# A hybrid mixer and expert network: context first, all its experts gathered row by row, value rows summed on PE

## The chip, the cores and the metric

The kernel runs on one core of one Trainium2 chip. The metric is the device time of one execution in microseconds, the median of the runs.

## The reference

Two layers act on 256 latent tokens `x` and 256 context tokens `ctx`, of 1024 channels each. A layer has a mixer and a PEER block. The second layer updates the latents only; its context enters through the keys and values.

```python
def mixer_sublayer(x, ctx, mod_x, mod_c, lp, rope, update_ctx):
    hx = modulate(rmsnorm(x, lp['g_norm1']), sh, sc)
    hc = modulate(rmsnorm(ctx, lp['g_norm1']), csh, csc)
    k_c, v_c = mla_kv(hc @ lp['w_in'][:, :KV_IN], lp, None)
    k_x, v_x = mla_kv(hx @ lp['w_in'][:, :KV_IN], lp, rope)
    ...
    a_x = latent_attention(q_x, concat(k_c, k_x), concat(v_c, v_x))
    x = x + gt * branch_merge(a_x, zf_x, zc_x, zg_x, lp)   # attention, FFT, convolution
    if update_ctx:
        a_c = softmax_attend(mla_q(cq_c, lp, None), k_c, v_c)
        ctx = ctx + cgt * branch_merge(a_c, zf_c, zc_c, zg_c, lp)

def peer_ffn(h, w_query, sub_keys, u_tab, v_tab):   # per token
    q = h @ w_query                                  # 8 heads x 2 x 64
    ...                                              # top 16 of 128 x 128 keys per head
    act = gelu(dot(u_tab[eid], h)) * softmax(best)   # 128 experts of 16384 a token
    return sum(act * v_tab[eid])
```

In layer 0 the context's mixer reads nothing of the latents, so it can go first; the latents' attention needs the context's keys and values.

## The kernel before

Channels lie on the partitions, tokens on the free axis; the residual `xT` and the normed input `hT` (a high and a low part) hold 512 columns, the context's 256 ahead of the latents' 256. Every weight tile of 512 KB is loaded by `raw` (SP's queue), rounded to its high part by ACT (`whi`, L237) and its low part is made by POOL, or by DVE for every third tile (`wlo`, L243). `mm3` (L257 to L259) does three matmuls for each chunk of 128.

The program runs in this order. `mixer(0)` does both streams at once, with 512 columns to a matmul: norm, convolution input, projections, keys and queries (`keys`), attention (`attend`), the branches' merge (`merge1`) and the output projection (`project`). The modulation (`adaln`, 12 parts; a part loads 4 MB in four tiles `wm` and multiplies each in four matmuls of 32 output columns, tile `ada`) is woven into the mixers: 2 parts first, 6 more in layer 0's mixer, 4 in layer 1's. Then `peer(0)`: queries, and for each of the four token tiles of 128 `retrieve` (L781), the top-16 search on DVE. Each token has 128 chosen experts. For the first token tile (`GATHER`) the chosen rows are fetched: `rows` (L856) lets POOL issue an indirect DMA for each of the 128 slots, 128 rows of 4 KB at a time, first of `u_tab`, which DVE multiplies with the token's input and sums (`dot`, L888; against `hnear` in PSUM, or `htok` in SBUF later), then of `v_tab`, which DVE scales and adds to `acc` (L901). There are five row buffers. The other 384 tokens are computed densely, all 16384 experts for each: `dense_u` computes scores tile by tile (`su`; 92 of 128 expert tiles are written to memory, the rest is computed in the value stage), `gates` builds a matrix of gate weights from one-hot products (`pw`, L951), and `dense_v` multiplies scores and gates (`xa`, L1028; split to `xh`, `xl` in L251 and L252) and sums the value rows in PSUM (`yacc`, six banks). Layer 1's mixer has 256 latent columns and 512 keys, and its PEER is dense for the 256 latents.

What sets the order: `weave` (L1059) interleaves generators by counts, and the counts stand in tables (`SPILL`, `END`, `PREP`, `FETCH`). A scheduler then orders each engine's instructions; `behind` and `pace` keep fetches and dots from moving ahead of the dense work that they were written beside.

Of the kernel before, what the change touches and what calls it, by code (L numbers as in the profile page):

```python
# [21 lines left out]
D = 1024  # L22
# [20 lines left out]

GATHER = (128, 0)
# [102 lines left out]
def body(ctx: ExitStack, tc, nc, a, out):  # L149
# [8 lines left out]
    pss = ctx.enter_context(tc.tile_pool(name="pss", bufs=2, space=PSUM))  # L158
    dram = ctx.enter_context(tc.tile_pool(name="dram", bufs=1, space=DRAM))


    last = ExitStack()
    banks = []

    def more_banks():
        last.close()
        psh = last.enter_context(pool_("psh", 2, space=PSUM))
        banks[:] = [ps, ps, psh, psh]

    def fewer_banks():  # L170
        last.close()
        banks[:] = [ps]
        return last.enter_context(pool_("psn", space=PSUM))
# [5 lines left out]
    ctx.callback(last.close)  # L179
    more_banks()  # L180
# [3 lines left out]

    def sm(name="sm"):
        return pss.tile([P, 512], F32, name=name, tag="sm")
# [46 lines left out]
    def split(r, n=D, lo_eng=None):  # L233
# [6 lines left out]
        if lo_eng is None:  # L240
            turn[0] += 1
            lo_eng = V if turn[0] % 3 == 0 else G
# [68 lines left out]
    def adaln(l, parts, pool, depth):  # L311


        acc = tp("ada")
# [102 lines left out]
    def head_norm_rope(pool, src, g, tile_idx, rope, name):  # L417

        sq = pool.tile([P, H, QKH], F32, name=name + "_hsq", tag="hsq", bufs=2)
# [7 lines left out]
        if rope:  # L427
# [3 lines left out]
            r = pool.tile([P, H, ROPE], F32, name=name + "_rot", tag="hrot", bufs=1)  # L431
# [20 lines left out]
    ADA1 = (6, 4, 4, 2, 4)  # L452

    def mixer(l, lay):
        both = l < L - 1
        streams = (0, 1) if both else (1,)
        q0 = 0 if both else NS
        nT = T - q0
        wt = a["wt"][l]
        macc = lay.tile([P, 8, nT], F32, name="macc")  # L460
        bra = lay.tile([P, 4, nT], F32, name="bra")
        bs = [lay.tile([P, 4, nT], F32R, name="bs%d" % k) for k in range(2)]

        def proj(i, cols=(q0, T), src=None, n=P):
            r = raw(wt[i] if src is None else src, 8 * n)
            w = split(r, 8 * n)
            p = mm("proj")
            for c in range(8):
                mm3(p[:n, :cols[1] - cols[0]], chunk(w, c, n), part(hT, c, cols), c == 0, c == 7)
            return p  # L470

        def gate(i):

            pz = proj(i)
            sg = lay.tile([P, nT], F32, name="gate", tag="gate", bufs=3)
            S.activation(out=sg, in_=pz[:, :nT], func=AF.Tanh, scale=0.5)
            return sg

        def branch(w, k0, x, xc, nk):
            pb = mm("pb")  # L480
            for k in range(nk):
                mm3(pb[:, :nT], chunk(w, k0 + k), part(x, xc + k, (0, nT)), k == 0, k == nk - 1)
            return pb[:, :nT]

        def conv(cp, up):
            cv = cp.tile([P, 2, nT], F32, name="cv")
            ns = len(streams)
            for c in range(2):
                o = cv[:, c].rearrange("p (s t) -> p s t", s=ns)
                for k in range(CW):  # L490
                    src = up[:, c, streams[0]:, k:k + NS]
# [6 lines left out]
            for c in range(2):  # L498
                PE.matmul(pmn[:, :nT], lhsT=ones, rhs=cv[:, c], start=c == 0, stop=c == 1)
            yield  # L500
            for c in range(2):
                V.scalar_tensor_tensor(out=cv[:, c], in0=pmn[:, :nT], scalar=-1.0 / 256, in1=cv[:, c], op0=ALU.mult, op1=ALU.add)
            ss = squares(cp, lambda c: cv[:, c], 2, nT, "cln")
            yield
            rs = tokstat(cp, ss, nT, 1.0 / 256, "cln")
            yield
            bc = spread(cp, rs, nT, "cln")
            for c in range(2):
                V.tensor_tensor(out=cv[:, c], in0=cv[:, c], in1=bc[:, :nT], op=ALU.mult)
# [3 lines left out]
        def fourier(fp, zf):  # L513
# [4 lines left out]
            for s in streams:  # L518
                for c in range(2):
                    o = s * NS - q0  # L520
                    zz = fp.tile([P, 2, 2, P], F32, name="zz", bufs=2)
                    for t in range(2):
                        p = mm("zc")
                        PE.matmul(p[:, :2 * P], lhsT=zf[:, c, o + t * P:o + (t + 1) * P], rhs=dftc, start=True, stop=True)
                        S.copy(out=zz[:, t], in_=p[:, :2 * P].rearrange("p (a b) -> p a b", a=2))
                    p = mm("zt")
                    for k in range(4):
                        PE.matmul(p[:, :NS], lhsT=zz[:, k // 2, k % 2], rhs=dftt[:, k // 2, k % 2], start=k == 0, stop=k == 3)
                    split_to(bs[0][:, c, o:o + NS], bs[1][:, c, o:o + NS], p[:, :NS])
                    yield  # L530
# [15 lines left out]
        def latents(ki, tmp):  # L546

            ckv = ki.tile([P, T], F32, name="ckv")
            kr = ki.tile([P, T], F32, name="krt")
            cq = ki.tile([P, 2, nT], F32, name="cq")  # L550
            p = proj(W_CKV, (0, T))
            ss = tmp.tile([P, T], F32, name="ckv_ss", tag="sq")
            S.activation(out=ss, in_=p, func=AF.Square)
            S.activation(out=ckv, in_=p, func=AF.Identity, scale=gckv[:, l])
            yield
            p = proj(0, (0, T), a["w_kr"][l], ROPE)
            S.copy(out=kr[:ROPE], in_=p[:ROPE])
# [646 lines left out]
```

## Time and profile before

| | |
|---|---|
| median of 3 runs | 2885.29 us (2884.65 to 2888.88) |
| profiled execution | 2882.8 us, its span 2881.0 us |
| mean granted clock | 0.981 |
| DMA | 675.67 MB, 235 GB/s in the mean |
| ACT busy | 1206.3 us, 42% |

Durations below come from the profiled execution, which is 2.5 us under the median. A matmul's listed duration is longer than the distance from its start to the next one's, since matmuls are pipelined; the distance is what counts. A matmul of plain 32-bit numbers shows as two records.

### The profile page before, as it was taken

The numbers are of one execution on the slowest core, as the hardware profiler recorded it, in microseconds if no ns is written. First come the engines' busy times: TensorE is split into PE (matmuls) and PEld (weight loads), VectorE is DVE, ScalarE is ACT, GpSimd is POOL, SyncE is SP. The second block draws the span as 40 slices with busy tenths as digits, with TensorE's granted clock in tenths as the row PEclk, the third lists the DMA queues.
The fourth block names the chain that finished last, engine by engine and source line by source line (L and its number), as shares of the span: only waits on it lengthen the run. The fifth ranks groups of instructions, "written<-read, shape, count | busy, mean of one in ns | idle before, by whom it ended". The sixth has DMA issues, their size and how long they took to land.

```text
span 2881.0 us, 43347 instructions
## 1 busy us (share of the span) xinstructions
PE 2741.1 (95%) x16144; PEld 2391.0 (83%) x16144; DVE 2170.9 (75%) x3907; ACT 1206.3 (42%) x1940; POOL 1498.0 (52%) x789
## 2 busy tenths in 40 slices
PE   7889999978999999999999998899999999999999
PEld 3467679877999998998788886678898999998887
DVE  4665437999989728999999996865398965667665
ACT  2144435432434443333333333455444554445543
POOL 2232235564666658899655563435443436665443
PEclk9999999988999999999999999999999999999999
DMA  8622144465778769999999995235465768667884
GB/s 330 249 73 80 37 132 132 154 217 200 288 269 296 284 245 354 323 319 316 366 354 349 352 321 219 92 110 209 148 204 197 249 226 291 211 206 254 292 291 141
DMA packets 263347, 675.67 MB, mean 235 GB/s; under 512 B 20192, under 2 KB 109408, under 8 KB 260320
## 3 DMA queue, kind: packets, MB, share of 16 engines
q1 hardware_dynamic: 210720, 467.63, 47.9%
q0 software_dynamic: 36864, 134.23, 12.7%
q10 hardware_dynamic: 15552, 71.05, 6.5%
q8 instruction: 126, 2.06, 0.3%
q14 instruction: 85, 0.70, 0.1%
HBM read 600.74 MB, written 72.09 MB: 234 GB/s over the span
## 4 chain that ended last, share of the span: by engine, by line
PE 77%; DVE 14%; DMA 4%; issue 2%; ACT 1%; POOL 1%; SPq 0%; DVEq 0%; ACTq 0%; POOLq 0%
PE yacc L257 10%; PE yacc L258 10%; PE yacc L259 10%; PE su L257 8%; PE su L259 8%; PE su L258 8%; PE pw L951 5%; PE proj L257 3%; PE proj L258 3%; PE proj L259 3%; PE ada L324 1%; DVE oh L827 1%; DVE wlo L243 1%; PE sc L628 1%; PE po L652 1%
## 5 line engine op out<-in xcount | busy, mean ns | idle before, releaser
L243 POOL TENSOR_TENSOR wlo<-wraw,whi 128x1024 fp32r<-128x1024 f32 (+1 forms) x466 | 1115.8, 2399 | 1055.1 <-ACT whi L237 1024.3
L237 ACT CAST whi<-wraw 128x1024 fp32r<-128x1024 f32 (+2 forms) x676 | 676.5, 1006 | 710.7 <-PE su L258 344.7
L257 PE MATMUL su<-hT,whi 128*128 128x384 f32 (+1 forms) x2048 | 643.7, 314 | 17.6 <-ACT psc L794 14.2
L259 PE MATMUL su<-hT,wlo 128*128 128x384 f32 (+1 forms) x2048 | 638.2, 312 | 11.8 <-DVE wlo L243 9.3
L258 PE MATMUL su<-hT,whi 128*128 128x384 f32 (+1 forms) x2048 | 640.0, 313 | 0.0
L257 PE MATMUL yacc<-whi,xh 128*128 128x512 f32 x1280 | 498.1, 390 | 7.6 <-ACT xh L251 7.6
L258 PE MATMUL yacc<-wlo,xh 128*128 128x512 f32 x1280 | 499.9, 391 | 0.0
L259 PE MATMUL yacc<-whi,xl 128*128 128x512 f32 x1280 | 497.0, 390 | 0.4 <-DVE xl L252 0.4
L257 PEld LDWEIGHTS su<-hT,whi 128*128 128x128 f32 x2048 | 393.4, 192 | 22.5 <-ACT psc L794 14.7
L259 PEld LDWEIGHTS su<-hT,wlo 128*128 128x128 f32 x2048 | 392.1, 192 | 13.5 <-DVE wlo L243 9.7
L243 DVE TENSOR_TENSOR wlo<-wraw,whi 128x1024 fp32r<-128x1024 f32 x210 | 305.4, 1455 | 129.9 <-ACT whi L237 126.3
L258 PEld LDWEIGHTS su<-hT,whi 128*128 128x128 f32 x2048 | 393.4, 192 | 3.0
L251 ACT CAST xh<-xa 128x384 fp32r<-128x384 f32 (+1 forms) x256 | 117.6, 460 | 585.8 <-DVE xa L1028 264.7
L257 PEld LDWEIGHTS yacc<-whi,xh 128*128 128x128 f32 x1280 | 240.6, 188 | 56.6 <-ACT xh L251 8.9
L259 PEld LDWEIGHTS yacc<-whi,xl 128*128 128x128 f32 x1280 | 240.4, 188 | 51.2 <-DVE xl L252 1.4
L258 PEld LDWEIGHTS yacc<-wlo,xh 128*128 128x128 f32 x1280 | 240.6, 188 | 47.9 <-POOL wlo L243 0.4
L252 DVE TENSOR_TENSOR xl<-xa,xh 128x384 fp32r<-128x384 f32 (+1 forms) x256 | 203.4, 796 | 94.9 <-ACT xh L251 94.7
L901 DVE SCALAR_TENSOR_TENSOR acc<-rows,act,acc 128x1024 f32<-128x1024 f32 x127 | 236.6, 1863 | 6.2 <-DMA rows<-in_v_tab,eidi 5.5
L862 POOL DMA_INDIRECT rows<-in_v_tab,eidi x128 | 160.2, 1252 | 154.2 <-DVE acc L901 119.5
L257 PE MATMUL proj<-hT,whi 128*128 128x512 f32 (+2 forms) x544 | 195.0, 361 | 14.0 <-ACT hT L251 10.0
L1028 DVE TENSOR_TENSOR xa<-snew,wrd 128x256 f32<-128x256 f32 (+1 forms) x80 | 132.0, 1652 | 92.3 <-ACT snew L1004 59.1
L259 PE MATMUL proj<-hT,wlo 128*128 128x512 f32 (+2 forms) x544 | 188.7, 347 | 1.2 <-POOL wlo L243 1.2
(273 smaller groups left out, 4226.1 us busy)
## 6 DMA issues: line engine op xcount, KB each, us to landing
wraw<-in_u_t SPq DMA_DIRECT2D x256, 512.0 KB, 4.3
wraw<-in_v_tab SPq DMA_DIRECT2D x256, 512.0 KB, 5.4
wraw<-in_wt SPq DMA_DIRECT2D x114, 512.0 KB, 3.8
wm<-in_w_mod SPq DMA_DIRECT2D x48, 1024.0 KB, 7.0
wd<-wst ACTq DMA_DIRECT2D x20, 2048.0 KB, 8.9
wrd<-wd SPq DMA_DIRECT2D x32, 768.0 KB, 11.1
sd<-sst ACTq DMA_DIRECT2D x46, 384.0 KB, 3.7
srd<-sd SPq DMA_DIRECT2D x46, 384.0 KB, 6.4
```

What stands on the lines that cost most here:

```text
L237: ins = S.copy(out=hi[:, :n], in_=r[:, :n])
L243: ins = lo_eng.tensor_tensor(out=lo[:, :n], in0=r[:, :n], in1=hi[:, :n].bitcast(F32), op=ALU.subtract)
L251: S.copy(out=hi, in_=src)
L252: return eng.tensor_tensor(out=lo, in0=src, in1=hi.bitcast(F32), op=ALU.subtract)
L257: PE.matmul(dst, lhsT=wh, rhs=xh, start=first, stop=False)
L258: PE.matmul(dst, lhsT=wh, rhs=xl, start=False, stop=False)
L259: return PE.matmul(dst, lhsT=wl, rhs=xh, start=False, stop=last)
L324: PE.matmul(acc[32 * g:32 * g + 32], lhsT=cond[:, c + g // 2, 6 - 2 * k:38 - 2 * k], rhs=w[:, g // 2, g % 2 * 512:(g % 2 + 1) * 512], star ...
L862: ins = G.indirect_dma_start(out=r, out_offset=None, in_=a[tab], in_offset=bass.IndirectOffsetOnAxis(ap=eid[:, k:k + 1], axis=0))
L901: return V.scalar_tensor_tensor(out=acc, in0=v, scalar=act[:, k:k + 1], in1=acc, op0=ALU.mult, op1=ALU.add)
L951: ins = PE.matmul(pw[:, t * NK:(t + 1) * NK], lhsT=oj[:, :, t], rhs=gg[:, k, :, t], start=k == 0, stop=k == 1)
L1028: V.tensor_tensor(out=x.rearrange("p (g t) -> p g t", t=TG), in0=got.pop(i).rearrange("p (g t) -> p g t", t=TG), in1=w[:, :, i % WB], op=A ...
```

## The change

1. `mixer` does one stream. Layer 0's context goes first, alone, with the ten parts of the modulation that are not needed ahead of it beside it (`run_beside` and `tick`: a step of the other work for so many microseconds of PE work, by the table `RATE`). Then the latents' mixer, beside which stand the context's queries, the retrieval of the first context tile and its 128 fetches of U rows. All weights of layer 0's mixer are loaded and split twice.
2. All 256 context tokens are gathered, two tiles of 128; the 256 latents alone are dense in layer 0, with 112 expert tiles of scores written to memory in place of 92, and four `yacc` banks. The second context tile's queries and inputs are kept in memory until the score stage retrieves it.
3. One chain `fetch` runs beside everything from the score stage on: V rows of tile 0, U rows of tile 1 (in the value stage, dots against SBUF), V rows of tile 1 (in the first part of layer 1's mixer). While gathers may run, `split` gives no low part to DVE by its every-third rule.
4. V rows are fetched by token: a DMA brings the 128 chosen rows of one token, and PE sums them (`gather_v`, `vacc`): for each pair of tokens four matmuls of 32 output columns, one for each token and half of the channels; `zd` holds a token's activations in one of 32 columns and zeros in the others, so each token's sum lands in a row of its own. DVE's additions are gone.
5. Layer 1's mixer does the latents' part first; `turn_to` then finishes the fetch, and only then come the context's norm, its keys and the attention.

The diff, cut to its core:

```diff
-            lo_eng = V if turn[0] % 3 == 0 else G
+            lo_eng = V if turn[0] % 3 == 0 and "Pool" not in pace else G
...
-    def mixer(l, lay):
-        both = l < L - 1
-        streams = (0, 1) if both else (1,)
+    def mixer(l, s, lay, keys_of, kv, start, turn_to=None, home=None):
+        q0 = s * NS
+        own = (q0, q0 + NS)
...
+            if turn_to is not None:
+                weave((m1, 16))
+                drain(m1)
+                turn_to()
+                with pool_("nrm") as np_:
+                    rs = norm_stat(0, np_, (0, NS), G)
+                    weave((m2, 4))
+                    norm_mod(l, 0, np_, (0, NS), rs)
...
-    def gather_v(l, gp, c0, res):
+    def gather_v(l, gp, zd, units):
-        def add(k, v):
-            if k == 0:
-                return V.tensor_scalar(out=acc, in0=v, scalar1=act[:, 0:1], scalar2=None, op0=ALU.mult)
-            return V.scalar_tensor_tensor(out=acc, in0=v, scalar=act[:, k:k + 1], in1=acc, op0=ALU.mult, op1=ALU.add)
-        yield from rows(gp, "v_tab", res["eidi"], add)
...
+        for m in range(len(seq) + 4):
+            if m < len(seq):
+                u, n = seq[m]
+                at = token(u, n)
+                q[m] = fetch(gp, "v_tab", turned(u)[0][:, at:at + 1])
+            if m >= 4 and m % 2 == 0 and m - 4 < len(seq):
+                u, n = seq[m - 4]
+                r = n // 2
...
+                for g in range(2):
+                    for half in range(2):
+                        o = 32 * (2 * half + g)
+                        one = PE.matmul(
+                            acc[o:o + 32], lhsT=zd[:, g, 32 * r:32 * r + 32], rhs=q[m - 4 + g][:, half * 512:(half + 1) * 512],
+                            start=r == 0, stop=r == 31,
+                        )
+                        first = pace.get("PE") if g == half == 0 else one_before
+                        if first:
+                            behind(one, first)
+                        one_before = one
...
-    SPILL = (92, 84)
+    SPILL = (112, 84)
+    END = (8, 16)
+    PREP = (196, 164)
...
-                weave((dv, NK - count), (fetch, FETCH[1]))
-                weave((dv, count), (fetch, 2 * (NR + LAG) - sum(FETCH) + FEND))
-                drain(fetch)
+                if "fetch" in beside:
+                    beside["fetch"][1] = RATE["value"]
+                dense_v(l, vp, vs, early, cols, count, sd, wd)
...
+    RATE = dict(front=0.5, x=0.85, score=0.37, value=0.46, last=1.0)
...
+                mixer(0, 0, lay, (0,), kv, start_context)
+                finish_beside("ada")
...
+                    run_beside("fetch", chain(retrieve(rp, qT, skt, ciota, 0, own[0]), gather_u(0, gp, own[0], lambda: t)), RATE["x"])
...
+                mixer(0, 1, lay, (1,), kv, start_latents, home=(0, NS))
+                finish_beside("fetch")
...
+        run_beside("fetch", chain(gather_v(0, gp, zd, units[0]), until_known(), gather_u(0, gp, own[1], token), gather_v(0, gp, zd, units[1])), RATE["score"])
+        peer(0, more)
+    def turn_to():
+        finish_beside("fetch")
+        after.close()
+        held[0] = False
+        pace.clear()
+            mixer(1, 1, lay, (0, 1), {}, start_last, turn_to)
```

Three places in the order of instructions. The first is POOL in layer 1's mixer around the context's norm (`n_ssq`) and its input (`hT`). Before:

```order
L359 TENSOR_TENSOR n_ssq<-n_ssq,n_sq 128x256
L252 TENSOR_TENSOR hT_84<-hn,hT_83 128x256
L243 TENSOR_TENSOR wlo<-wraw,whi 128x1024 x3
L252 TENSOR_TENSOR hT_84<-hn,hT_83 128x256
L243 TENSOR_TENSOR wlo<-wraw,whi 128x256
L252 TENSOR_TENSOR hT_84<-hn,hT_83 128x256 x3
L243 TENSOR_TENSOR wlo<-wraw,whi 128x1024 x3
L243 TENSOR_TENSOR wlo<-wraw,whi 128x256
```

In the changed kernel:

```order
L588 TENSOR_TENSOR macc<-macc,gate 128x256
L280 TENSOR_TENSOR wlo<-wraw,whi 128x1024
L897 DMA rows<-in_v_tab,idsT 128x1024 x43
L396 TENSOR_TENSOR n_ssq<-n_ssq,n_sq 128x256 x7
L289 TENSOR_TENSOR hT_87<-hn,hT_86 128x256 x4
L280 TENSOR_TENSOR wlo<-wraw,whi 128x256 x2
L462 TENSOR_TENSOR ktok<-ktok,gqkc 128x768
```

The norm moved behind the whole fetch of V rows (`rows<-in_v_tab`), the last 43 of which stand one after another on POOL; the splits that stood among the norm's steps come after it.

The second is PE at the same place, in the changed kernel alone; `vacc` are the value rows' matmuls, `pb` a branch's projection and `n_ss`, `n_bc` the context's norm:

```order
L296 MATMUL pb<-bs_17462,wlo 128x256
L294 MATMUL pb<-bs_17462,whi 128x256
L295 MATMUL pb<-bs_17463,whi 128x256
L296 MATMUL pb<-bs_17462,wlo 128x256
L971 MATMUL vacc<-rows,zd 32x512 x98
L987 MATMUL ypt<-pack,yvg 128x128 x4
L403 MATMUL n_ss<-pack,n_ssq 128x1 x2
L414 MATMUL n_bc<-n_dg,pack 128x128 x2
L294 MATMUL proj<-hT_86,whi 128x512
```

A run of 98 value-row matmuls now stands between the last branch matmul and the context's norm. Elsewhere they stand in blocks of two or four among scores and projections.

The third is DVE in layer 0's value stage, where a value tile's split (`wlo`), the product with the gates (`xa`, `xl`) and one row's work alternate. Before:

```order
L243 TENSOR_TENSOR wlo<-wraw,whi 128x1024
L901 SCALAR_TENSOR_TENSOR acc<-rows,act,acc 128x1024
L252 TENSOR_TENSOR xl<-xa,xh 128x384
L1028 TENSOR_TENSOR xa<-srd,wrd 128x384
L901 SCALAR_TENSOR_TENSOR acc<-rows,act,acc 128x1024
L252 TENSOR_TENSOR xl<-xa,xh 128x384
```

In the changed kernel:

```order
L280 TENSOR_TENSOR wlo<-wraw,whi 128x1024
L923 SCALAR_TENSOR_TENSOR rows,act<-rows,htok 128x1024
L1119 TENSOR_TENSOR xa<-snew,wrd 128x256
L289 TENSOR_TENSOR xl<-xa,xh 128x256
L923 SCALAR_TENSOR_TENSOR rows,act<-rows,htok 128x1024
L1119 TENSOR_TENSOR xa<-snew,wrd 128x256
```

The additions of V rows (`acc`) are gone from here; in their place stand dots with U rows of the second context tile (`htok`), and the dense rows are 256 wide.

## Rows read from the trace of the kernel before

**Rows 1.** The page's first part: busy us, share of the span, instructions.

```profile
PE 2741.1 (95%) x16144; PEld 2391.0 (83%) x16144; DVE 2170.9 (75%) x3907; ACT 1206.3 (42%) x1940; POOL 1498.0 (52%) x789
```

**Rows 2.** Busy time by stage, PE PEld DVE ACT POOL, then PEclk, DMA share, GB/s.

```profile
0.00:480.00 480.00, 434.74 (x2266) 314.09 (x2267) 263.87 (x544) 186.52 (x350) 148.44 (x79) 0.98 0.43 148
480.00:539.00 59.00, 55.45 (x431) 53.42 (x431) 48.02 (x176) 29.74 (x55) 27.90 (x15) 0.97 0.46 147
539.00:1084.00 545.00, 511.57 (x3167) 494.67 (x3165) 452.78 (x1187) 209.27 (x313) 315.63 (x177) 0.96 0.70 250
1084.00:1758.00 674.00, 666.54 (x3120) 572.77 (x3121) 638.81 (x578) 235.75 (x330) 468.10 (x271) 1.00 0.93 331
1758.00:2037.00 279.00, 252.65 (x1746) 204.29 (x1745) 193.08 (x416) 136.46 (x271) 118.38 (x75) 0.96 0.44 153
2037.00:2881.00 844.00, 820.13 (x5424) 751.78 (x5419) 574.33 (x1009) 408.56 (x621) 419.50 (x174) 0.99 0.68 229
```

**Rows 3.** The same columns for a stretch inside the value stage.

```profile
1500.00:1700.00 200.00, 200.00 (x884) 165.74 (x883) 198.42 (x173) 71.89 (x98) 113.28 (x72) 1.00 0.99 353
```

**Rows 4.** Timeline of PE where scores end and values follow: start, duration.

```profile
1142.94 0.33 PE L259 MATMUL su<-hT,wlo 128*128 128x384 f32 x1
1143.12 0.39 PE L257 MATMUL yacc<-whi,xh 128*128 128x512 f32 x1
1143.35 0.40 PE L258 MATMUL yacc<-wlo,xh 128*128 128x512 f32 x1
```

**Rows 5.** Timeline of PE in the last PEER's scores, 256 columns.

```profile
2083.04 0.28 PE L257 MATMUL su<-hT,whi 128*128 128x256 f32 x1
2083.16 0.28 PE L258 MATMUL su<-hT,whi 128*128 128x256 f32 x1
```

**Rows 6.** Timeline of PE at a modulation block in layer 0's mixer.

```profile
86.64 0.39 PE L257 MATMUL proj<-hT,whi 128*128 128x512 f32 x1
86.96 1.06 PE L324 MATMUL ada<-wm,cond 128*32 128x512 f32 x8
87.95 0.50 PE L258 MATMUL proj<-hT,whi 128*128 128x512 f32 x1
```

**Rows 7.** Timeline of PE at a shorter modulation block, layer 1's mixer.

```profile
1763.80 1.05 PE L324 MATMUL ada<-wm,cond 128*32 128x512 f32 x4
1764.78 0.48 PE L385 MATMUL n_cs<-n_sq,pack 128*128 128x256 f32 x1
```

**Rows 8.** The chain that ended last, in the scores: start, duration.

```profile
690.72 1.89 PE pw L951 x16
```

**Rows 9.** Groups of DVE's instructions in the value stage (1084 to 1758).

```profile
L901 DVE SCALAR_TENSOR_TENSOR acc<-rows,act,acc 128x1024 f32<-128x1024 f32 x127 | 236.6, 1863 | 6.2 <-DMA rows<-in_v_tab,eidi 5.5
L243 DVE TENSOR_TENSOR wlo<-wraw,whi 128x1024 fp32r<-128x1024 f32 x64 | 122.9, 1920 | 4.5 <-ACT whi L237 4.5
L252 DVE TENSOR_TENSOR xl<-xa,xh 128x384 fp32r<-128x384 f32 x128 | 91.5, 716 | 3.8 <-ACT xh L251 3.7
L888 DVE SCALAR_TENSOR_TENSOR rows<-rows,htok 128x1024 f32<-128x1024 f32 x53 | 86.7, 1661 | 4.1 <-DMA rows<-in_u_tab,eidi 4.1
L1028 DVE TENSOR_TENSOR xa<-srd,wrd 128x384 f32<-128x384 f32 x92 | 68.7, 749 | 2.3
```

**Rows 10.** Group of DVE's dots against PSUM, over the whole run.

```profile
L888 DVE SCALAR_TENSOR_TENSOR rows<-rows,hnear 128x1024 f32<-128x1024 f32 x75 | 90.6, 1209 | 6.3 <-DMA rows<-in_u_tab,eidi 6.1
```

**Rows 11.** Groups of POOL's instructions in the value stage (1084 to 1758).

```profile
L243 POOL TENSOR_TENSOR wlo<-wraw,whi 128x1024 fp32r<-128x1024 f32 x95 | 242.6, 2556 | 13.5 <-issue 7.8 <-ACT whi L237 3.8
L862 POOL DMA_INDIRECT rows<-in_v_tab,eidi x128 | 160.2, 1252 | 154.2 <-DVE acc L901 119.5 <-ACT whi L237 12.1 <-issue 7.9
L862 POOL DMA_INDIRECT rows<-in_u_tab,eidi x48 | 65.3, 1360 | 17.2 <-issue 6.4 <-DVE rows L888 4.9 <-DMA wraw<-in_v_tab 3.7
```

**Rows 12.** Timeline of POOL where two gathers follow each other.

```profile
1199.68 1.30 POOL L862 DMA_INDIRECT rows<-in_u_tab,eidi  x1 [0.30 <-issue]
1201.28 1.30 POOL L862 DMA_INDIRECT rows<-in_u_tab,eidi  x1 [0.30 <-issue]
```

More of the change, by code (lines that the diff above doesn't have):

```diff
@@ L698, in mixer @@
-                weave((fourier(fp, zf), 4 if both else 2), (ada, 16 if both else ADA1[4]), (cvg, 38))
+                    S.copy(out=zf[:, c], in_=p[:, :NS])
+                fourier(fp, zf)
                 order.clear()
-                lat = []
-                lt = latents(ki, fp)
-                while not lat:
-                    try:
-                        next(lt)
-                    except StopIteration as e:
-                        lat = e.value
-                    weave((ada, 6), (cvg, 1))
@@ L762, in mixer @@
-            drain(project(streams[0], not both))
-            if both:
-                rest = project(1)
-                weave((rest, 1))
-                rs = norm_stat(1, mp, (0, NS))
-                weave((rest, 2))
-                norm_mod(l, 1, mp, (0, NS), rs)
-                drain(rest)
+                split_to(*mixed(f), sg)
+            cs = slice(*own)
+            if (l, s) == (0, 0):
+                rs = norm_stat(0, mp, (NS, T), G)
+            for f in range(8):
+                w = split(raw(wt[W_OUT + f]))
+                p = mm("po2")
+                for c in range(8):
+                    mm3(p[:, :NS], chunk(w, c), mixed(c), c == 0, c == 7)
+                tick(2.9)
+                V.scalar_tensor_tensor(out=xT[:, f, cs], in0=p[:, :NS], scalar=mod[:, l, 16 + f, s:s + 1], in1=xT[:, f, cs], op0=ALU.mult, op1=ALU.add)
+                if f:
+                    pending()
+                else:
+                    pm = tp("n1_cs")
+                sq = mp.tile([P, NS], F32, name="n1_sq", tag="n1_sq", bufs=2)
+                pending = col_square(sq, pm[:, :NS], xT[:, f, cs], f == 0, f == 7)
+                if f == 2 and (l, s) == (0, 0):
+                    norm_mod(0, 0, mp, (NS, T), rs)
@@ L920, in gates @@
             yield
-        tab = pss.tile([P, 4, 2 * P], F16, name="gtab", tag="sm")
+        tab = table([P, 4, 2 * P], F16, "gtab")
         for k in range(4):
@@ L1085, in chain, with make_queries @@
             yield from g
-    SPILL = (92, 84)
-    def peer(l):
-        c0 = 0 if l < L - 1 else NS
-        n, g = T - c0, GATHER[l]
-        cols = (c0 + g, T)
+    SPILL = (112, 84)
+    END = (8, 16)
+    PREP = (196, 164)
+    CONV_RATE = 2.4
+    def make_queries(l, qT, cols):
+        for h in range(H):
+            w = split(raw(a["wt"][l][W_QRY + h]))
+            p = mm("pq")
+            for c in range(8):
+                ins = mm3(p[:, :NS], chunk(w, c), part(hT, c, cols), c == 0, c == 7)
+            if "PE" in pace:
+                pace["PE"] = ins
+            tick(2.9)
+            S.copy(out=qT[:, h], in_=p[:, :NS])
+            yield
@@ L1153, in peer @@
-                weave((du, 4), (got[0], 8 if g else 0))
-                fetch = iter(())
-                if g:
-                    drain(got[0])
-                    fetch = chain(gather_u(l, gp, c0, res[0]), gather_v(l, gp, c0, res[0]))
-                weave((du, count - END[l]), (prep, PREP[l]), (fetch, FETCH[0]))
+                sd = dram.tile([count // 2, P, 2, n], F32, name="sd%d" % l)
+                wd = dram.tile([n // TG, NK, NK, TG], F32, name="wd%d" % l)
+                res = [results(rp, t) for t in range(2)]
```

670 lines of the change are left out of this document (381 added, 289 removed).

## The prediction

> **What bounds the kernel now.** I read the page's first part, then the busy time by stage, then single rows of a stage for the price of each kind of work. The page gives PE 95% of a span of 2881.0 us, DVE 75%, POOL 52% [rows 1]. That average hides three different situations, and the stage table shows them [rows 2]. In layer 0's mixer, the queries and layer 1's mixer (818 us of the span) the DMA share is under a half and POOL is busy about a third of the time; PE pays for its waits there. In layer 0's expert scores and in the last PEER, PE works and the rest has slack. In layer 0's value stage (674 us) everything is near its end: PE 666.54, DVE 638.81, DMA share 0.93 at 331 GB/s. A quiet stretch inside it has PE busy for all of 200 us, DVE for 198.42, the rings at 0.99 and 353 GB/s [rows 3]. So a saving of PE work alone buys little in that stage, while the mixers have room on POOL and the rings. The change takes dense work from PE and pays with gathers in the mixers. The question is what a gather costs where it is put.
>
> **What it removes from PE.** Dense columns of layer 0 go from 384 to 256. A score matmul goes from 0.18 us start to start (1143.12 - 1142.94, [rows 4]; 0.173 over the dozen rows ahead of it) to 0.12 (2083.16 - 2083.04, [rows 5]); 128 experts x 24 of them = 3072, with 0.173 and 0.120 -163 us. A value matmul of 512 columns takes 0.23 (1143.35 - 1143.12, [rows 4]; 0.227 over longer runs of the same rows); 128 experts x 2 banks x 3 = 768 fewer, -174. The one-hot products cost 1.89 us for 16 [rows 8], and one token tile of three (256) goes: -30. Together -367 us.
>
> **What it adds to PE.** The mixer's projections run as two of 256 columns in place of one of 512: 0.240 for 0.227, +14 over the mixer. The value rows of 256 tokens are 128 pairs x 4 matmuls of 32 columns. No such row exists before; the nearest is the modulation's 32-column matmul. A block of four of them (eight records) sits between two projections that start 87.95 - 86.64 = 1.31 apart, where one without it takes 0.23: 1.08 for the block [rows 6]. A block of two (four records) takes 0.98 from its start to the next [rows 7]: half the work, nearly the same price. So I count blocks. In the order of the changed kernel the 512 value-row matmuls stand in 139 short blocks, two thirds of them of only two, and 150 more matmuls stand in long blocks worth 38 fours: 177 x 1.08 = +191 us. If each pair of rows went in one block it would be 128 x 1.08 = 138; if the columns' tiles did not overlap at all, about twice my figure. I take 191, since the rows of two and of four stand nearest to it. PE's net is -367 + 14 + 191 = -162.
>
> The Trainium skill, TensorEngine Tiling (Array Packing), Key Properties, has a rule that speaks against such interleaving: changing the tiling mode drains the TensorE. By its table of speedups alone (up to 4x for 32 columns) the sum would be 138; with the drain at each block it is the 191 above. The block of two that costs as much as a block of four agrees with the drain.
>
> **What it moves on the other engines.** DVE loses 127 additions of 1.863 us and gains 128 dots, and its dense work shrinks by a third; its total hardly changes, but the stages do. POOL gains 256 gathers: 1.25 us mean as V rows, 1.36 as U rows beside dots [rows 11], 1.6 start to start when they queue back to back (1201.28 - 1199.68, [rows 12]): +320 to +410 us. The rings carry 256 gathers more of 512 KB (134 MB), and the mixer's weights twice (24 MB), less some 30 MB of scratch traffic. The gathers' queue is POOL's own, in program order with the splits of the weights: a gather that has no buffer holds up the split behind it, and PE waits for that split. Beside the gathers no split goes to DVE any more.
>
> **Stage by stage, against the profiled execution** (2882.8 us, 1.8 over its span; the median of the runs is 2.5 higher).
>
> A, the context's mixer alone. Layer 1's mixer, also 256 columns, takes 279 [rows 2]. A has all 12 modulation parts and that stage has 4: 8 x 4 blocks x 1.08 = +35. The context attends to half the keys, which is worth between nothing and as much again; I take half back: A = 297.
>
> B, the latents' mixer with the context's queries and 128 U gathers. Layer 1's mixer without modulation is 279 - 17 = 262, and queries are 59, half of its retrievals included: 321 if nothing else limits. DVE: 193 + 48 [rows 2], less some 25 splits that move to POOL, 25 x 1.9 [rows 9], plus about 100 dots at 1.209 + 0.08 [rows 10] = 322. POOL: 118 + 25 splits x 2.56 + 100 gathers at 1.25 to 1.6 [rows 11, 12] = 307 to 342. Three engines near 320 that wait for one another do not give 320. Layer 1's mixer had PE at 0.91 of its time [rows 2]; DVE so makes 354 and POOL's upper count 376. I take B = 370, nearer to POOL's, since its gathers wait for dots. A and B together are 667 where the two stages before took 539.
>
> C, scores. PE: 112 experts x 24 x 0.120 = 323, one-hot products 61, 93 blocks of value rows 100, 256 columns of queries 23, retrieval 11: 518. The stage before had 545 - 512 = 33 us of PE idle [rows 2], which the same retrievals cause; C = 550.
>
> D, values. PE: 1536 x 0.227 + 384 x 0.120 = 395. DVE: 119 dots x 1.74 + 64 splits x 1.92, and two thirds of the xl and xa rows, 128 x (0.716 + 0.749) x 2/3 [rows 9] = 455. DMA: 168 MB, 476 us at the 353 GB/s of [rows 3] and 508 at the 331 of the stage. The rings end it: D = 490, against 674. This is where the change earns its money.
>
> E, layer 1's mixer. 262 without modulation, 84 blocks of value rows 91, so PE alone makes 353. The order shows one run of 98 value-row matmuls with nothing between them, and ahead of the context's norm 43 gathers with one another for neighbours on POOL. The fetch of tile 1 is not done when the context's half of this mixer needs its columns, and the rest is drained there. 43 x 1.6 = 69 us, in which PE has 25 blocks, 27 us, to do: 42 more. E = 400 with 5 for the other gathers' delays, against 279.
>
> F, the last PEER, is not changed in size: 844.
>
> Sum: 297 + 370 + 550 + 490 + 400 + 844 = 2951, with 1.8 around the span 2953, and 2955 against the median: some 2.4% slower. C and D together give back 179 us; A, B and E take 249.
>
> **Rivals.** 1: faster. The gathers slip past the splits, so the engine with the most work paces each stage and nothing else: A 297, B 342 (POOL's upper count), C 518, D 476, E 353, F 844 = 2830, and 2834 against the median. For it: DVE reached 0.99 in the value stage while PE was full too [rows 3], so the order that the scheduler makes can be dense. Against: POOL's idle time ahead of the V gathers was 119.5 us of waiting for DVE to free a row buffer [rows 11]. It decides for this side if E comes out at its PE count, or B under 345 and D under 480. At best PE's whole net is kept: 2885 - 162 = 2723.
> 2: much slower. The gathers find no cover: 256 x 1.6 = 410 us more, less PE's 162 = 3133. For it: the gathers stand in stages with many short chains (attention, norms) where POOL's place in the order decides. Against: in the value stage before, 176 gathers ran with PE at 99% [rows 2].
> 3: no change to within 0.2%, some 6 us, about what a measurement of this kernel can tell from none: it needs D's gain and the mixers' loss to cancel by chance. Nothing in the rows asks for that.
> That the change does not do what it says is not a case of its own: the order shows the gathers beside both mixers, and the burst at the end of E is the part that does not fit.
>
> **How the numbers follow.** Forecast case, 2891 to 3060: 0.57. Rival 1, under 2879: 0.31. Rival 3: 0.04. Rival 2, over 3060: 0.08. The range takes rival 1 down to 2790 (0.07 lies below, at the PE-only end) and the forecast up to 3060: 2790 to 3060, 0.85 in it by these cases, with the unknown price of a block (138 to twice 191) inside. The likeliest case alone reaches from 2891 to 3060. Faster 0.31, same 0.04, slower 0.65.
>
> **What would show it.** PE busy near 2580 us and its share near 87%. Value-row blocks of two at about 1.0 us. In the value stage DVE and DMA ahead of PE. In layer 1's mixer a hole of some 40 us on PE whose chain runs through POOL's gathers. POOL busy about 1850. I am wrong if the mixers' two stages take less than 620 us together or the last mixer less than 340; then POOL's queue was no limit. I am wrong the other way if the value stage stays over 560.

## The result and the profile after

| | before | changed kernel |
|---|---|---|
| median of 4 runs | 2884.97 us | 3154.32 us (3147.75 to 3161.03) |
| ratio | 1 | 1.0931, 95% interval 1.0903 to 1.0958 |
| profiled execution, span | 2882.8, 2881.0 us | 3161.0, 3159.2 us |
| mean granted clock | 0.981 | 0.937 |

The change makes the kernel 9.3% slower. The forecast had the sign (2.4% slower) but missed the size; the time lies 94 us over the top of the range. The first part of the page:

```profile
PE 2764.0 (87%) x17230; PEld 2237.6 (71%) x17230; DVE 2149.3 (68%) x4180; ACT 1216.0 (38%) x2025; POOL 1763.3 (56%) x1102
```

Against [rows 1], DVE's total hardly moved, as forecast, and POOL has 265 us more, where 320 to 410 were counted. PE's busy time did not fall. In part that is the clock: a matmul counts as busy for longer where the granted clock is at its lower level. The query matmuls at 727 us, where the granted clock is 0.50, start 0.21 us apart and are listed with 0.41; in [rows 5] it is 0.12 and 0.28.

```profile
727.02 0.41 PE L294 MATMUL pq<-hT,whi 128*128 128x256 f32 x1
727.23 0.41 PE L295 MATMUL pq<-hT,whi 128*128 128x256 f32 x1
```

PE is busy for 265 us within stretches at the lower level, against 58 us before.

The rows of the next table are the forecast's stages A to F, cut at events of the trace (A ends where POOL clears the convolution's input a second time, B where the second tile's queries are read back, C at the first `yacc`, D behind the fourth copy of a `yacc` bank, E at the last PEER's first query matmul). Columns as in [rows 2]:

```profile
0.00:315.00 315.00, 279.75 (x1907) 201.33 (x1908) 173.72 (x394) 123.81 (x257) 115.09 (x78) 0.94 0.73 264
315.00:727.00 412.00, 290.76 (x1859) 254.73 (x1858) 349.17 (x799) 137.90 (x258) 270.86 (x202) 0.85 0.64 219
727.00:1311.00 584.00, 553.86 (x4054) 451.07 (x4053) 365.67 (x971) 216.55 (x336) 354.76 (x237) 0.97 0.86 306
1311.00:1850.00 539.00, 439.66 (x1867) 344.52 (x1867) 483.66 (x584) 192.08 (x285) 356.50 (x211) 0.91 0.92 323
1850.00:2309.00 459.00, 376.40 (x2150) 230.32 (x2148) 204.44 (x439) 138.95 (x272) 250.84 (x205) 0.92 0.61 207
2309.00:3159.00 850.00, 823.59 (x5400) 755.68 (x5400) 572.68 (x995) 406.73 (x619) 415.29 (x171) 0.98 0.67 226
```

| stage | A | B | C | D | E | F | sum |
|---|---|---|---|---|---|---|---|
| forecast | 297 | 370 | 550 | 490 | 400 | 844 | 2951 |
| measured | 315 | 412 | 584 | 539 | 459 | 850 | 3159 |

No stage is far out by itself; five of them miss by 18 to 59 us, all to the same side. So the question for the runs was whether one thing had been left out everywhere, or several.

In the value stage (D) PE's waits name the splits on POOL, and POOL's waits name DVE's dots. The first fence is the view of PE's waits there, the second POOL's (line waited for: us in total, times, longest):

```profile
PE yacc L295 <- POOL wlo L280: 49.5, 35, 3.8
PE vpt L940 <- DVE rows L923: 19.6, 1, 19.6
PE yacc L294 <- ACT whi L274: 15.0, 12, 1.3
```

```profile
POOL rows L897 <- DVE rows L923: 103.6, 65, 4.0
POOL wlo L280 <- ACT whi L274: 45.7, 24, 6.3
```

A timeline of all engines from the middle of that stage, here only the rows that matter, shows how one leads to the other:

```profile
1561.03 0.95 POOL L897 DMA_INDIRECT rows<-in_u_tab,ids  x1 [3.97 <-DVE rows L923]
1562.57 1.68 POOL L897 DMA_INDIRECT rows<-in_u_tab,ids  x1 [0.58 <-DVE rows L923]
1563.81 3.11 DVE L1119 TENSOR_TENSOR xa<-srd,wrd 128x256 f32<-128x256 f32 x1
1564.27 2.35 POOL L280 TENSOR_TENSOR wlo<-wraw,whi 128x1024 fp32r<-128x1024 f32 x1
1566.67 0.50 PE L295 MATMUL yacc<-wlo,xh 128*128 128x512 f32 x1 [3.82 <-POOL wlo L280]
1566.84 1.21 DVE L923 SCALAR_TENSOR_TENSOR rows<-rows,htok 128x1024 f32<-128x1024 f32 x1
1568.33 0.95 POOL L897 DMA_INDIRECT rows<-in_u_tab,ids  x1 [1.71 <-DVE rows L923]
1568.43 0.42 DVE L1119 TENSOR_TENSOR xa<-srd,wrd 128x256 f32<-128x256 f32 x1
1568.77 4.00 DVE L280 TENSOR_TENSOR wlo<-wraw,whi 128x1024 fp32r<-128x1024 f32 x1
1569.30 2.38 POOL L280 TENSOR_TENSOR wlo<-wraw,whi 128x1024 fp32r<-128x1024 f32 x1
```

The 19.6 us of `vpt` in PE's waits are one wait, at the stage's end, for the last dot. In the timeline, the gather at 1561.03 had waited 3.97 us for a row buffer; the split in the queue behind it starts at 1564.27, and PE waits 3.82 us for it. While POOL makes that split, DVE's product `xa` takes 3.11 us and ends 0.3 us behind it, where the one at 1568.43, with POOL on a gather, takes 0.42. A split on DVE that meets one on POOL takes 4.00. So DVE's next dot comes late, its buffer is freed late, and POOL's next gather waits, and with it the next split: POOL and DVE wait for each other in turn, and PE waits for POOL.

### The profile page after: what moved, and what is told of

Read it like the earlier page. It is cut to its first block, busy times and chain, and to the rows that moved or that the text cites. A ratio compares the mean times of both kernels' runs of the same rounds, so it can differ in the third digit from the quotient of the medians.

```text
span 3159.2 us, 46780 instructions
## 1 busy us (share of the span) xinstructions
PE 2764.0 (87%) x17230; PEld 2237.6 (71%) x17230; DVE 2149.3 (68%) x4180; ACT 1216.0 (38%) x2025; POOL 1763.3 (56%) x1102
## 5 line engine op out<-in xcount | busy, mean ns | idle before, releaser
L280 POOL TENSOR_TENSOR wlo<-wraw,whi 128x1024 fp32r<-128x1024 f32 (+2 forms) x502 | 1153.5, 2303 | 898.7 <-ACT whi L274 784.5
L274 ACT CAST whi<-wraw 128x1024 fp32r<-128x1024 f32 (+1 forms) x734 | 720.0, 988 | 676.7 <-PE su L295 235.3
L294 PE MATMUL su<-hT,whi 128*128 128x256 f32 x2048 | 597.2, 292 | 13.5 <-ACT psc L833 5.1
L296 PE MATMUL su<-hT,wlo 128*128 128x256 f32 x2048 | 590.4, 289 | 16.7 <-DVE wlo L280 8.6
L295 PE MATMUL su<-hT,whi 128*128 128x256 f32 x2048 | 584.5, 285 | 0.0
L897 POOL DMA_INDIRECT rows<-in_u_tab,ids x256 | 274.1, 1071 | 175.4 <-DVE rows L923 120.0
L897 POOL DMA_INDIRECT rows<-in_v_tab,idsT x256 | 256.8, 1003 | 156.3 <-PE vacc L971 101.1
L971 PE MATMUL vacc<-rows,zd 128*32 128x512 f32 x1024 | 235.8, 627 | 38.3 <-DMA rows<-in_v_tab,idsT 37.9
L294 PE MATMUL proj<-hT,whi 128*128 128x256 f32 (+1 forms) x816 | 248.0, 306 | 17.5 <-ACT hT L288 7.4
L296 PE MATMUL proj<-hT,wlo 128*128 128x256 f32 (+2 forms) x816 | 242.8, 299 | 7.6 <-POOL wlo L280 5.6
L295 PE MATMUL proj<-hT,whi 128*128 128x256 f32 (+2 forms) x816 | 241.1, 296 | 0.0
```

Source lines behind the costliest of these rows:

```text
L274: ins = S.copy(out=hi[:, :n], in_=r[:, :n])
L280: ins = lo_eng.tensor_tensor(out=lo[:, :n], in0=r[:, :n], in1=hi[:, :n].bitcast(F32), op=ALU.subtract)
L294: PE.matmul(dst, lhsT=wh, rhs=xh, start=first, stop=False)
L295: PE.matmul(dst, lhsT=wh, rhs=xl, start=False, stop=False)
L296: return PE.matmul(dst, lhsT=wl, rhs=xh, start=False, stop=last)
L897: ins = G.indirect_dma_start(out=r, out_offset=None, in_=a[tab], in_offset=bass.IndirectOffsetOnAxis(ap=ids, axis=0))
```

## The experiments

Four theories stand in the expectations. R: the DMA rings are full, and a gather costs its bytes. P: a gather costs its place in POOL's queue. V: DVE is full. S, formed after the first eight runs: a split on POOL keeps DVE waiting, as in the timeline above. Stage lengths of all are at the end of this section.

**Bytes, dots, splits, and no gathers at all.** The first halves every row that a gather brings:

```diff
-        ins = G.indirect_dma_start(out=r, out_offset=None, in_=a[tab], in_offset=bass.IndirectOffsetOnAxis(ap=ids, axis=0))
+        ins = G.indirect_dma_start(out=r[:, :512], out_offset=None, in_=a[tab].rearrange("n (b c) -> (n b) c", b=2), in_offset=bass.IndirectOffsetOnAxis(ap=ids, axis=0))
```

with dots and value rows reading the half twice, so that their sizes stay.

> Every gather brings 2 KB of each row in place of 4 KB (the other half of the row is left out of the sums); the instructions of all engines keep their number, order and size. Theory R (the DMA rings are full from the first U gather to the last V gather, so each gather costs its 512 KB at about 331 GB/s, 1.55 us, wherever it stands): 512 gathers carry 134 MB less, 405 us of ring time, of which the other engines' own work lets through perhaps half: 2900 to 3020 us, the DMA share of that stretch well under 0.8, the 98-matmul run in layer 1's mixer near 50 us in place of 78, and the GB/s lower. Theory P (a gather costs the place that its instruction takes in POOL's queue, and what waits behind it): the queue is the same, so 3120 to 3160 us. Theory V (DVE's dots pace the value stage): the value stage stays at 520 to 531 us.

Measured: 3104.94 us, 49 less. The run of 98 value-row matmuls, with the gathers alone on the rings, went from some 76 to 70 us, while the rings' share fell from 0.94 to 0.66. The stretch in the changed kernel, then here:

```profile
2024.00:2100.00 76.00, 53.16 (x210) 9.90 (x208) 0.86 (x2) 1.62 (x3) 50.39 (x52) 0.96 0.94 331
```

```profile
1970.00:2040.00 70.00, 51.07 (x206) 8.03 (x204) 1.71 (x2) 1.73 (x3) 49.92 (x51) 0.95 0.66 193
```

With a third of the rings' time free, the stretch moves by 8%. A ring share of 0.94 had looked like the limit, and something else holds the stretch near 70. R falls as the main cause; that the rings set the pace at 0.94, with the next limit 6 us behind, is not excluded for this stretch. Theory P's bound (3120 or more) is missed by 15 us.

The second cuts the dots to 32 channels (`in0=u[:, :32]`, `in1=ht[:, :32]`).

> Each dot with a U row takes 32 of its 1024 channels (the rest is left out of the sum), so DVE has some 300 us less to do in the latents' mixer, the scores and the value stage; fetches and PE are the same. Theory R: the value stage moves its 172 MB at the same rate and keeps 510 to 531 us; the whole is 3060 to 3140, with what is gained in the latents' mixer, where the rings are half idle for its first 200 us. Theory V: the value stage falls to some 440 us, and the whole to 3000 or less. Theory P: row buffers come free sooner, POOL's 104 us of waiting for dots go, and the value stage falls to some 450 us.

Measured: 3102.69 us, 52 less, 46 of them in D (493). The whole lies in R's range, D under it (510 to 531) and well over what V and P said (440 to 450). The third undoes one line of the change:

```diff
-            lo_eng = V if turn[0] % 3 == 0 and "Pool" not in pace else G
+            lo_eng = V if turn[0] % 3 == 0 else G
```

> Undoes one line: while gathers may run, every third split's low part goes to DVE again. Theory P (POOL's queue holds up splits): the latents' mixer gets some 30 us shorter, layer 1's mixer some 15, the whole 3090 to 3120. Theory R: splits move no bytes; 3140 to 3165, or a little longer where DVE is nearly full.

Measured: 3148.23 us, no change that can be told, where P said 3090 to 3120. B is 15 shorter, D 13 longer. The fourth takes the fetches away.

> Leaves out all fetches, dots and value rows of the 256 context tokens (their expert sums stay out of the result); their queries and retrievals stay. It shows the rest of the change bare: context first, weights twice, 256 dense columns. By the counts of the prediction without gathers: context's mixer 297, latents' mixer 321, scores 445, values 400, layer 1's mixer 265, last PEER 844: 2575 us. Theory R and theory P both say that the 580 us between this and the changed kernel are the gathers'; a much longer bare kernel (over 2750 us) would put the loss on the new order of the mixers instead.

Measured: 2679.63 us. The 512 gathers cost 475 us with all that belongs to them, 0.93 each; and the bare kernel is 105 us longer than my counts for it. Both halves of the forecast were short, by about the same.

**What of a gather costs.** Two kernels take away one part after another: first bytes and dots (rows of 32 channels, dots of 32), then the value rows too.

> Gathers bring 32 of 1024 channels, and the dots take those 32 (the rest stays out of the sums; the value rows read the 32 channels sixteen times over). What is left of a gather is POOL's instruction and PE's value-row blocks; bytes (137 MB) and dot time (some 330 us of DVE) are gone. Half the bytes alone gave 49 us and the dots alone 52. Theory P (POOL's instructions and the queue): value stage 470 to 490, whole 3020 to 3070. Theory R+V (bytes and dots together pace it and cover each other): value stage 400 to 420, whole below 2950.

> As thin_dots, and of each 32 pairs only the first has its value-row matmuls; a copy of 32 channels on DVE frees the other rows (their sums stay out). What is left of a gather is POOL's instruction alone. Against 2680 with no gathers: theory P says the 512 instructions keep most of the cost, 2850 or more (512 x 0.4 us or more); if PE's blocks and their waits were the cost, 2680 to 2760, with scores near 470 and layer 1's mixer near 330.

Measured: 2986.16 and 2896.99 us, one run each. From no gathers upward: POOL's 512 instructions, with a sliver of bytes and dots, +217 (0.42 us each), PE's value rows +89, bytes and dots together +168. So in time the value rows are worth under half of the 191 us that were counted for them. In the first D is 465, between the two expectations; the second is in P's range. A part of the instructions' own cost is waits for splits: in B, PE waits for them in the projections, 23.1 us there against 3.9 in the kernel without gathers (PE's waits of thin_pool, then of no_gather). That is 19 us of the 81 by which the two stages differ; the rest is not traced.

```profile
PE proj L296 <- POOL wlo L280: 23.1, 10, 7.9
```

```profile
PE proj L296 <- POOL wlo L280: 3.9, 5, 1.1
```

Bytes and dots gave 49 and 52 alone, but 168 together; the thin rows also carry fewer bytes than the half ones. Either the two cover each other, or the second half of the bytes is worth more than the first; no run parts these.

The other way round, plain loads on SP's queue in place of POOL's instructions, all else kept:

```diff
-        ins = G.indirect_dma_start(out=r, out_offset=None, in_=a[tab], in_offset=bass.IndirectOffsetOnAxis(ap=ids, axis=0))
...
+        ins = SP.dma_start(out=r, in_=a[tab][at:at + P])
...
```

> Every gather becomes a plain load of 128 neighbouring rows (so the wrong ones) of the same 512 KB, issued by SP's queue: bytes, dots, value rows and row buffers stay, POOL has 512 instructions less. Theory P: 2900 to 3000, the value stage near 440. Theory R or V: 3080 to 3150, the value stage 520 or more. SP's queue is in order, so a load that waits for a row buffer may hold up weight tiles; then PE waits for whi's loads, and the run tells little on P.

Measured: 3110.20 us, one run; P's range is missed, R's and V's is met. C, D and E are 34, 38 and 21 us shorter, B is 42 longer, where PE now waits 53 us for query heads that DVE makes (`q_pt`). D is at 501, so taking POOL's gathers away is not enough there; something else holds DVE. The run tells little on B, as feared.

**The order of layer 1's mixer.** The edit, made on the kernel without gathers:

```diff
+        rs = norm_stat(0, np_, (0, NS), G)
         norm_mod(1, 0, np_, (NS, T), bc=rsb)
+        norm_mod(1, 0, np_, (0, NS), rs)
+        turn_to()
...
-            mixer(1, 1, lay, (0, 1), {}, start_last, turn_to)
+            mixer(1, 1, lay, (0, 1), {}, start_last)
```

> Without gathers, and with layer 1's mixer in the order of the kernel before (context's norm ahead, keys of both streams from the start). In the bare kernel this mixer took 316 us, where I had 262 to 265. If the new order of that mixer is what costs, it takes 260 to 275 here and the whole is near 2630; if not, it stays at 310 or more and the whole at 2680.

Measured: 2637.67 us, one run, that mixer 277 in place of 316. So 39 us belong to the latents-first order by itself. The waits of PE that it adds are small and many, 67 us in all against 29: with the context's norm in the middle, PE waits 6.7 us for its spreading (`n_bc`) and 6.4 for the first key's heads (`k_pt`), where the old order has 2.6 and 2.1, and the mixer's granted clock is 0.86 where the old order has 0.91.

**Who keeps DVE busy in D.** The table of DVE's groups in D, in the changed kernel (mean ns behind the busy us):

```profile
L923 DVE SCALAR_TENSOR_TENSOR rows<-rows,htok 128x1024 f32<-128x1024 f32 x128 | 188.6, 1483 | 7.3 <-DMA rows<-in_u_tab,ids 7.1
L289 DVE TENSOR_TENSOR xl<-xa,xh 128x256 fp32r<-128x256 f32 x126 | 121.8, 969 | 24.9 <-ACT xh L288 23.1 <-PE yacc L296 1.2 <-issue 0.5
L280 DVE TENSOR_TENSOR wlo<-wraw,whi 128x1024 fp32r<-128x1024 f32 x64 | 109.0, 1703 | 7.3 <-ACT whi L274 7.0
L1119 DVE TENSOR_TENSOR xa<-srd,wrd 128x256 f32<-128x256 f32 x112 | 66.3, 597 | 2.5
```

Theory S says these means hold waits for POOL. The single rows of the stage say the same. Of DVE's splits, products and dots, 117 overlap a split on POOL, and 74 of these are longer than the shortest of their kind, by 163 us together; of the 327 others none is. It goes both ways: POOL's splits take from 2.34 to 3.38 us, and the 18 over 2.85 all began while a split or a dot was under way on DVE and ended 2.2 to 2.3 us behind its end. And it takes two operands in SBUF: of the 128 dots of the first context tile, whose second operand lies in PSUM, 57 overlap a split on POOL, and none takes over 1.22 us. Their group in B:

```profile
L923 DVE SCALAR_TENSOR_TENSOR rows<-rows,hnear 128x1024 f32<-128x1024 f32 x102 | 122.5, 1211 | 13.4 <-DMA rows<-in_u_tab,ids 12.5 <-issue 0.7
```

The test gives DVE more work: all splits of the stage.

```diff
-                scores(l, i, cols, p, G)
+                scores(l, i, cols, p, V if l == 0 else G)
...
-            v = split(r, lo_eng=V if i % 2 else G)
+            v = split(r, lo_eng=V if i % 2 or l == 0 else G)
```

> In layer 0's value stage all low parts of the weights are made on DVE; POOL does nothing there but its gathers. In the changed kernel DVE is busy for 481 of the stage's 531 us, but 164 us of that are excess of instructions that overlap a split on POOL (a product xa takes 3.1 or 0.42 us, a split 4.0 or 1.2). Theory S (a split on POOL keeps DVE's instructions with two SBUF operands waiting, DVE's dots then free row buffers late, and POOL's queue waits for those buffers): DVE needs 128 x 1.29 + 128 x 1.22 + 126 x 0.84 = 427 us and the stage falls to 450 to 480, the whole to 3070 to 3100. Theory V (DVE is simply full): 64 splits more at 1.70 are 109 us more, the stage goes to 600 or more and the whole over 3210.

Measured: 3068.95 us, ratio to before 1.0643 (1.0613 to 1.0674), and D 447 in place of 539, both just under theory S's ranges (3070 to 3100, and 450 to 480) and far from V's 3210. DVE does 76 splits more there and is busy 75 us less. Stage D and its groups in this kernel:

```profile
1309.00:1756.00 447.00, 409.85 (x1868) 327.41 (x1869) 408.19 (x659) 192.23 (x283) 142.21 (x129) 0.98 1.02 382
```

```profile
L280 DVE TENSOR_TENSOR wlo<-wraw,whi 128x1024 fp32r<-128x1024 f32 x140 | 168.4, 1222 | 14.0 <-ACT whi L274 12.2
L923 DVE SCALAR_TENSOR_TENSOR rows<-rows,htok 128x1024 f32<-128x1024 f32 x128 | 155.6, 1225 | 3.9 <-DMA rows<-in_u_tab,ids 3.8
L289 DVE TENSOR_TENSOR xl<-xa,xh 128x256 fp32r<-128x256 f32 x126 | 53.0, 423 | 10.4 <-ACT xh L288 9.8
L1119 DVE TENSOR_TENSOR xa<-srd,wrd 128x256 f32<-128x256 f32 x112 | 47.1, 424 | 2.5
```

```profile
POOL rows L897 <- DVE rows L923: 297.7, 106, 11.9
```

The same instructions take 1225, 423, 1222 and 424 ns. Against the changed kernel that is 128 x 0.258 + 126 x 0.546 + 64 x 0.481 + 112 x 0.173 = 152 us of waiting that its DVE rows contained. The last fence is POOL's wait for row buffers: nearly three times as long as in the changed kernel, in a stage that is 92 us shorter. Nothing is queued behind those gathers any more, so the wait costs nothing. And the rings move 382 GB/s.

The edit does two things at once: DVE is no longer held, and no split stands behind a gather. sp_fetch does the second alone, with the splits still on POOL, and has 38 of the 92 us. So the effect of both together is shown, and the share of each only roughly.

> The same from the latents' mixer to the end of the gathers: every split there on DVE. Theory S with a queue: POOL has some 230 splits (570 us) less ahead of its gathers. The value stage as in dve_value; the latents' mixer 380 to 420, since DVE is its fullest engine; scores 540 to 570; layer 1's mixer 440 to 450: 3010 to 3070. Theory V: 3200 or more.

Measured: 3037.97 us, ratio 1.0536 (1.0505 to 1.0567). Beyond dve_value the scores gained (556 for 588) and layer 1's mixer 11 us; the latents' mixer stayed at 406, and the value stage came out 15 us longer than in dve_value, at 462, which was not expected.

**The same lock in the kernel before.** Its value stage shows the same stretched rows [rows 9].

> The kernel before, with only the splits of layer 0's value stage all on DVE. There 224 us of DVE's 639 are excess of instructions that overlap a split on POOL, but PE has 663 us of matmuls in the 674 of the stage. Theory S says the lock is the same, and that it costs only where DVE or POOL paces: DVE falls to some 540 us, the stage to 664 to 672, the whole by 2 to 10 us (ratio 0.997 to 0.999). A gain of over 1% would say that the lock also held PE up in the kernel before.

> The same in both value stages. In the last PEER PE has 806 us of matmuls in 844, most of the rest in its scores and retrieval, so its value stage has little to give: between no change and 8 us less than before_dve0.

Measured: 2876.32 us, ratio 0.9972 (0.9960 to 0.9985), and 2874.34 us, ratio 0.9962 (0.9948 to 0.9976): a few microseconds shorter than the kernel before, as theory S said for a stage that PE fills. The value stage, to be held against the fourth of [rows 2]:

```profile
1084.00:1750.00 666.00, 666.00 (x3140) 572.89 (x3138) 536.53 (x671) 239.50 (x329) 225.27 (x176) 1.00 0.93 334
```

DVE took on POOL's splits and is busy 102 us less; PE is now busy for the whole stage, 8 us shorter than before.

| stage, us | A | B | C | D | E | F | median |
|---|---|---|---|---|---|---|---|
| changed kernel | 315 | 412 | 584 | 539 | 459 | 850 | 3154 |
| half_rows | 311 | 440 | 529 | 528 | 442 | 849 | 3105 |
| small_dots | 311 | 399 | 593 | 493 | 458 | 848 | 3103 |
| dve_splits | 309 | 397 | 585 | 552 | 459 | 849 | 3148 |
| sp_fetch | 312 | 454 | 550 | 501 | 438 | 854 | 3110 |
| thin_dots | 310 | 421 | 532 | 465 | 408 | 848 | 2986 |
| thin_pool | 310 | 422 | 496 | 449 | 370 | 848 | 2897 |
| no_gather | 310 | 341 | 463 | 397 | 316 | 851 | 2680 |
| ng_order | 311 | 341 | 462 | 400 | 277 | 845 | 2638 |
| dve_value | 309 | 412 | 588 | 447 | 463 | 848 | 3069 |
| dve_all | 309 | 406 | 556 | 462 | 452 | 849 | 3038 |

The line between B and C moves by some tens of microseconds with the time at which the second tile's queries are read back; of half_rows only the sum of B and C (969 for 996) should be read.

## Why the prediction was wrong, point by point

**PE's work: the price of a block was right, its reason and its weight were not.** A block of value rows costs what the modulation's blocks of [rows 6] and [rows 7] do. The timeline of PE in the scores: two matmuls for one token of a pair, 0.98 us to the next start.

```profile
902.36 0.28 PE L296 MATMUL su<-hT,wlo 128*128 128x256 f32 x1
902.57 1.05 PE L971 MATMUL vacc<-rows,zd 128*32 128x512 f32 x4
903.55 0.38 PE L294 MATMUL su<-hT,whi 128*128 128x256 f32 x1
```

That a block of two costs as much as one of four was read as a drain at each block. The rows give another reason. In the kernel before, a block of one matmul (two records) takes 0.97 us to the next start, one of four 0.99 [rows 6], and one of twelve 2.72:

```profile
1765.85 1.04 PE L324 MATMUL ada<-wm,cond 128*32 128x512 f32 x2
1766.82 0.48 PE L385 MATMUL n_cs<-n_sq,pack 128*128 128x256 f32 x1
```

```profile
74.39 2.78 PE L324 MATMUL ada<-wm,cond 128*32 128x512 f32 x24
77.11 0.50 PE L257 MATMUL proj<-hT,whi 128*128 128x512 f32 x1
```

So up to four matmuls of 32 columns run side by side in one price, four more add 0.87, and what a block pays for its two changes of shape is at most some 0.12 us (0.99 - 0.87). In the forecast's count the 191 us come from blocks that are half empty, not from a drain. And as time the value rows were worth 89 us (thin_dots against thin_pool, one run each).

"PE busy near 2580" was wrong as a sign: it came out at 2764. Some 90 of the 184 us more are the lower clock's, an estimate from 207 us more of busy time at that level and 0.21 us for 0.12; the rest is not traced.

**A and F: right** to within 18 and 6 us. The bare terms of B and C (341 and 463 without gathers, where 321 and 445 were counted) are 20 and 18 short, and not followed further.

**D: the step that failed is "The rings end it: D = 490".** D took 539, with the rings at 323 GB/s and a share of 0.92, near the 331 GB/s and 0.93 of that step. But nearly the same bytes went through in 447 us, at 382 GB/s, when POOL's splits moved to DVE. The 331 GB/s and 0.93 of [rows 2] were no ceiling of the rings; they were what a stage asked for that something else paced. The "something else" was in the rows that I used as prices: 1.92 us for a split on DVE and 1.66 for a dot [rows 9] held the waits for POOL, and I read them as DVE's work. The prediction had even named the wait (a gather that has no buffer holds up the split behind it, and PE waits for that split), and gave it no time in D. The better reading was in [rows 9] against [rows 10], a dot at 1661 ns with its second operand in SBUF and at 1209 in PSUM: with two operands in SBUF it can be held by POOL. The Trainium skill, GPSIMD Engine Reference, Specifications, states that POOL's SBUF interfaces are shared with VectorE and that DVE instructions with two SBUF inputs contend with it. The runs agree, with 3.11 against 0.42 us for one product, and add the price: 152 us of DVE's time in this stage.

**E: the step that failed is "262 without modulation".** The bare mixer in its new order takes 316, and 277 in the old one. That the fetch would not be done in time, and would end in a run of 98 matmuls fed by 43 gathers, was right; the run took 76 us where 69 were counted. What gathers add to E, 143 us (459 - 316), is near the 138 of the forecast (91 + 42 + 5), but by luck: the thin runs split it otherwise, POOL's instructions 54, value rows 38, bytes and dots 51.

**B and C: the gathers' share was too small.** B pays 71 us for its gathers (412 - 341), and 81 with thin rows and thin dots, so neither bytes nor dots set it; and dve_all, which has no split on POOL there, still takes 406, so the splits that wait behind gathers are not the whole of it either. Of PE's listed waits in B, 119 us with gathers and 71 without, POOL's splits are 13 and 10. I had only DVE's and POOL's totals against each other there. What sets B in the end stays open: queries, retrieval, attention and gathers share short chains, and no run took these apart. C pays 121, where 105 were counted, 100 of them for value rows; by the thin runs these are 36, POOL's instructions 33, bytes and dots 52.

Summed up against the 2951: 105 us are the bare kernel's (39 of them the order of layer 1's mixer), about 100 are the gathers', half of that in D. The lock of POOL and DVE accounts for the miss in D and not for the sign: without it, in dve_all, the kernel is still 5.4% slower than before. Rival 2's 3133 came near the time, but not its mechanism: it let 256 gathers more cost 1.6 us of uncovered time each, and all 512 cost 0.93 each, from POOL's queue, PE's blocks, bytes and dots. Rival 1 was wrong at the same step as the forecast: it let every stage end with its fullest engine, and only F and C come near that (PE busy 824 of 850 and 554 of 584 us).

## What to carry to other kernels

A duration read in a stage where two engines share a resource is not a price: compare the shortest instance of an instruction with its mean, and look at what the other engine does while it is long. When two engines feed each other's buffers through in-order queues, moving all the work of one kind to the fuller engine can make both faster (D: 539 to 447 us, with DVE busy 75 us less), and a wait grows harmless once nothing stands behind it. A transfer share of 0.9 showed here that the rings were used, not that they paced; halve the bytes before calling it a bound.

## What the runs showed of the hardware

A split of 128x1024 on POOL (2.35 us alone) and a DVE instruction with two SBUF operands do not run side by side in D: DVE's took 3.11 for 0.42 us and 4.00 for 1.22, or, where DVE's had begun, POOL's took up to 3.38. DVE's dots against PSUM were not held (1.22 at most in 57 that overlap a split). Without such splits DVE's dots took 1225 ns against SBUF, nearly the 1209 of [rows 10] against PSUM. POOL's gathers do not do this: the products beside them take 0.42 us.

The rings moved 382 GB/s for 447 us (dve_value, D), over the 353 of [rows 3].

The granted clock stood at its lower level in 57 stretches of together 399 us, against 14 and 110 us in the kernel before. Of the 57, 44 lie in B, D and E, where PE waits often and briefly; with the waits of D gone (dve_value), that stage is at 0.98 in place of 0.91. What the lower clock cost by itself was not tried.
